# Gated linear attention in a two-layer decoder trunk: where four groups of small products stand in TensorE's queue, and where one scan stands in VectorE's

## The chip, the cores and the metric

The kernel runs on one core of one Trainium2 chip. The metric is the device time of one execution in microseconds (us); the lower, the better. The time quoted for a kernel is the median of its runs.

## The reference, cut to what matters

The reference is a causal decoder trunk of two layers on 512 tokens of 1024 features, in float32. Layer 0 mixes tokens by sliding-window attention and a short convolution, layer 1 by chunked gated linear attention (GLA); each layer then has a gated MLP with a convolution and a gated per-layer embedding. The change lies in the mixer of layer 1 alone:

```python
def _gla_mixer(h, w_in, w_gate_up, gate_bias, o_norm, w_out):
    q, k, v, g_lr, og = _split(h @ w_in, GLA_SPLITS)        # 512, 512, 1024, 16, 1024 columns
    log_a = log_sigmoid(g_lr @ w_gate_up + gate_bias) / 16
    o = _gla_chunked(heads(q) * 128 ** -0.5, heads(k), heads(v), heads(log_a))   # 4 heads, keys 128, values 256
    o = _rms_norm(o, o_norm) * silu(heads(og))
    return o.reshape(b, s, 1024) @ w_out

# within a head, for t >= s:  score[t, s] = sum_d q[t, d] k[s, d] exp(G[t, d] - G[s, d]),  G = cumsum(log_a)
# output[t] = sum_s score[t, s] v[s]
...
```

## The kernel before, in words

Everything is laid out with features or keys on the 128 partitions and the 512 tokens along the free dimension, or, for the values, with 128 tokens on the partitions. There are two kinds of product on TensorE.

The **large products** are the projections with `gla_w_in`. `mm3` (L159 to L165) computes one float32 product out of three with float32r parts: high times high, high times low, low times high. `weights` and `cut` (L118 to L145) load a block of weights and split it: ScalarE rounds it into `wh` (L143), VectorE subtracts to get the rest `wl` (L144). A feature of 128 columns takes 8 x 3 = 24 products of 512 columns into one PSUM bank named `ps`, of which there are four. `query(w, h)`, `key(w, h)` and `gate(w, m)` each make one such feature, and VectorE then copies it out of the bank with a multiplication (L1672, L1680, L1685). A class `Values` makes the values in two steps of 48 products of 336 or 352 columns.

The **small products** are what the attention itself needs, in plain float32, and go to four banks named `pa`. For each head `h`, in order:

- `base(h)`: the scan on VectorE that makes the running sum `G` (L1759), and a multiply of even keys and queries (L1765); GpSimd clears the scores `sc`.
- `diag(h)`: the diagonal, one product with ones (L1771), multiplied into `sc` by VectorE (L1772).
- `decay(h, levels)`, `decay_pairs(h)`, `decay_off(h)`: VectorE and ScalarE make the decay factors `F` of seven block sizes.
- `level(h, levels)`: the scores of each block size (L1806, L1809), merged into `sc` by VectorE; `lo` is the first four sizes, `hi` the fifth; `level_pairs(h)` the last two (L1844).
- `off(h)`: transposes for what passes from block to block (L1888); `state(h)`: the states (L1902), summed by VectorE (L1905).
- `read(h)`: the outputs (L1926, L1928), their squares on ScalarE (L1932), the power -1/2 on GpSimd (L173), and the scaling into `sc` by four multiplies on VectorE (L1936).
- `turn(h)`: eight transposes of the scaled rows (L1943), copied to `oT` by ScalarE (L1947). `gated(m)` then multiplies with the gate.

`load_vectors_ffn(1)` loads small vectors for the next MLP and transposes them with two products (L223).

The order is made in two steps. The program calls these functions in an order written out by hand at the end of `mixer1`; a planner then puts the instructions of each engine into one queue, by that order as priority and by when it expects their inputs. Small products are ready or not at their own times, so the planner puts them between, or in the middle of, the 24 products of a feature. Each engine works through its queue in order: an instruction that waits holds up all that stands behind it. `tc.issue_after(x)` ties what is written in its block, on `x`'s engine alone, to a place behind `x` in that queue; it adds no wait at run time.

In the built queue of before, `diag(0)` is a run of its own between `key(1)` and `query(2)`; `level(0, hi)` and `off(0)` are a run between `query(3)` and `key(2)`, and `level_pairs(0)` with `diag(1)` one between `key(2)` and `key(3)`. From `gate(w, 1)` on there are: `turn(1)` with the two transposes of vectors; `level(3, hi)` after 2 products of `gate(w, 2)`; `off(3)` after 4 more; `read(2)` with `level_pairs(3)` after 4 more; `turn(2)` with `state(3)` after the other 14; `read(3)` after the 24 products of `gate(w, 3)`.

Of the kernel before, what the change touches and what calls it, by code (L numbers as in the profile page):

```python
# [9 lines left out]
F32 = mybir.dt.float32  # L10
# [4 lines left out]
ALU = mybir.AluOpType  # L15
# [3 lines left out]
P = 128  # L19
# [3 lines left out]
ND = D // P  # L23
# [33 lines left out]
class Kernel:  # L57
# [69 lines left out]
    def cut(self, rv, by, at=(0, 0)):  # L127

        nc = self.nc
        na, nb = rv.shape[1:]  # L130
        parts = []
        n = 2 if na * nb > 1024 else 1
        for k in range(n):
            if by == "b":
                a, b = na, nb // n
                v = rv[:, :, k * b : (k + 1) * b]
            else:
                a, b = na // n, nb
                v = rv[:, k * a : (k + 1) * a, :]
            h, l = self.wide("wh", at[0]), self.wide("wl", at[1])  # L140
            hv = h[:, : a * b].rearrange("p (a b) -> p a b", b=b)
            lv = l[:, : a * b].rearrange("p (a b) -> p a b", b=b)
            nc.scalar.activation(hv, v, AF.Copy)  # L143
            nc.vector.tensor_tensor(lv, v, hv.bitcast(F32), ALU.subtract)  # L144
            parts.append((hv, lv))  # L145

        def get(i, c0, c1):
            if by == "b":
                b = nb // n
                k = c0 // b  # L150
                h, l = parts[k]
                return h[:, i, c0 - k * b : c1 - k * b], l[:, i, c0 - k * b : c1 - k * b]
            a = na // n
            h, l = parts[i // a]
            return h[:, i % a, c0:c1], l[:, i % a, c0:c1]

        return get

    def mm3(self, out, lt, rt, start, stop, **kw):  # L159

        mm = self.nc.tensor.matmul
        (lh, ll), (rh, rl) = lt, rt
        mm(out, lh, rh, start=start, stop=False, **kw)  # L163
        mm(out, lh, rl, start=False, stop=False, **kw)  # L164
        mm(out, ll, rh, start=False, stop=stop, **kw)  # L165

    def rsqrt(self, out, src, scale):

# [1455 lines left out]
    def mixer1(self):  # L1624
# [4 lines left out]
        with tc.tile_pool(name="m1", bufs=1) as mp:  # L1629
# [5 lines left out]
            class Values:  # L1635


                def __init__(v, c0, c1, vn):
                    v.c0, v.n, v.vn = c0, c1 - c0, vn
                    v.ws = [  # L1640
                        self.weights(w_in[:, k0 : k0 + 4, 1024 + c0 : 1024 + c1], 4, v.n, by="a") for k0 in (0, 4)
                    ]

                def step(v, i):
                    c0, n, vn = v.c0, v.n, v.vn
                    if i == 0:
                        v.pss = [self.ps() for _ in range(NT)]
                    for k in range(4 * i, 4 * i + 4):
                        for t in range(NT):
                            self.mm3(  # L1650
                                v.pss[t][:, :n], tok(k, t), v.ws[i](k % 4, 0, n), start=k == 0, stop=k == ND - 1
                            )
                    for t in range(NT if i else 0):
                        rt = r[:, t : t + 1]
                        if n > vn:
                            nc.scalar.activation(glr[:, t, :], v.pss[t][:, vn:n], AF.Copy, scale=rt)
                        nc.scalar.activation(vt[t][:, c0 : c0 + vn], v.pss[t][:, :vn], AF.Copy, scale=rt)
# [5 lines left out]

            def feature(w, c):
                ps = self.ps()
                for k in range(ND):
                    self.mm3(ps, w(k, c * P, (c + 1) * P), xg[k], start=k == 0, stop=k == ND - 1)
                return ps

            def query(w, h):  # L1670
                o = qT[h] = self.fp.tile([P, S], F32, tag="a0", name=self.nm("qT"))
                nc.vector.scalar_tensor_tensor(  # L1672
                    out=o, in0=feature(w, h % 2), scalar=float(GDK**-0.5), in1=R, op0=ALU.mult, op1=ALU.mult
                )
# [81 lines left out]
            def base(h):  # L1756

                G = Gs[h] = mp.tile([P, S], F32, tag="G", name=self.nm("G"), bufs=2)
                nc.vector.tensor_tensor_scan(  # L1759
                    G, run.rearrange("p a b -> p (a b)"), las[h], 0.0, op0=ALU.mult, op1=ALU.add  # L1760
                )
                sc = scores[h] = mp.tile([P, GDV * NT], F32, tag="sc", name=self.nm("sc"), bufs=3)

                pr = Fs[h, "diag"] = new()[:, : S // 2]
                nc.vector.tensor_tensor(pr, ev(kT[h]), ev(qT[h]), ALU.mult)  # L1765
                nc.gpsimd.memset(sc[:, :S], 0.0)

            def diag(h):
                sc = scores[h]
                pd = self.pa()[:, : S // 2]  # L1770
                mm(pd, self.ones, Fs[h, "diag"], start=True, stop=True)  # L1771
                nc.vector.tensor_tensor(  # L1772
                    sc[:, :S].rearrange("p (a n b) -> p a n b", a=NT, b=2)[:, :, :, 0],
                    pd.rearrange("p (a n) -> p a n", a=NT),
                    ev(self.ident).unsqueeze(1).to_broadcast([P, NT, P // 2]), ALU.mult,
                )
# [18 lines left out]
            def level(h, levels):  # L1795
                A = scores[h][:, :S]
                for l in levels:
                    b, F = LEVELS[l], Fs[h, l]
                    pl = self.pa()
                    for t in range(NT):  # L1800
                        c = slice(t * P, (t + 1) * P)
                        if b < 64:

                            for u in (0, 64):
                                d = slice(t * P + u, t * P + u + 64)
                                mm(second(pl[u : u + 64, d], b), F[:, d], second(F[:, d], b), start=True, stop=True)  # L1806
                        else:
                            mid = t * P + b
                            mm(pl[:b, mid : mid + b], F[:, t * P : mid], F[:, mid : mid + b], start=True, stop=True)  # L1809
                    if b < 64:  # L1810
                        for u in (0, 64):
                            r = slice(u, u + 64)
                            tv = lambda x: x.rearrange("p (t c) -> p t c", c=P)[r, :, r].rearrange(
                                "p t (n b) -> p t n b", b=2 * b
                            )[:, :, :, b:]
                            mk = second(msk[r, l, r], b).unsqueeze(1).to_broadcast([64, NT, 32 // b, b])
                            nc.vector.copy_predicated(tv(A), mk, tv(pl))
                    else:
                        nc.vector.tensor_copy(second(A[:b], b), second(pl[:b], b))
# [63 lines left out]
            def off(h):  # L1883

                Es, Ec, tot = Fs[h, "off"]
                pt = self.pa()
                for i in range(NT - 1):
                    nc.tensor.transpose(pt[:, i * P : (i + 1) * P], Es[:, i * P : (i + 1) * P], self.ident)  # L1888
                kt = new()
                nc.scalar.copy(kt[:, : 3 * P], pt[:, : 3 * P])  # L1890
                Fs[h, "kt"] = kt
# [46 lines left out]
            def turn(h):  # L1938
                o = scores[h]
                for m in range(2):  # L1940
                    pb = self.pa()
                    for t in range(NT):
                        nc.tensor.transpose(  # L1943
                            pb[:, t * P : (t + 1) * P], o[:, t * GDV + m * P : t * GDV + (m + 1) * P], self.ident
                        )
                    y = self.fp.tile([P, S], F32, tag="a1", name=self.nm("oT"))
                    nc.scalar.activation(y, pb, AF.Copy, scale=self.g_o[:, m : m + 1])  # L1947
                    oT[2 * h + m] = y
# [21 lines left out]
            key(w, 1)  # L1970
            w = pair_w(256)
            base(0)
            diag(0)
            decay(0, lo)
            query(w, 2)
            level(0, lo)
            decay(0, hi)
            decay_off(0)
            decay_pairs(0)
            query(w, 3)  # L1980
            w = pair_w(768)
            level(0, hi)
            off(0)
            base(1)
            decay(1, lo)
            key(w, 2)
            level_pairs(0)
            diag(1)
            key(w, 3)
            v = Values(0, 336, 336)  # L1990
            level(1, lo)
# [3 lines left out]
            v.step(0)  # L1995
            level(1, hi)
            off(1)
            base(2)
            decay(2, lo)
            v.step(1)  # L2000
            v = Values(336, 672, 336)
# [24 lines left out]
            decay_pairs(3)  # L2026
            state(2)
            gate(w, 1)
            turn(1)
            w = pair_w(2064 + 256)  # L2030
            self.load_vectors_ffn(1)
            level(3, hi)
            off(3)
            read(2)
            level_pairs(3)
            gate(w, 2)
            turn(2)
            state(3)
            gated(0)
# [52 lines left out]
```

## Time and profile before

| what | value |
|---|---|
| time, median of 3 runs | 1203.48 us (1203.18 to 1203.55) |
| the profiled execution's own time | 1202.58 us |
| its span, first to last instruction | 1200.8 us |
| TensorE busy with products | 1192.9 us, 99% |
| VectorE busy | 994.2 us, 83% |
| ScalarE busy | 685.2 us, 57% |
| GpSimd busy | 42.9 us, 4% |
| mean granted clock of TensorE | 0.999 |

In the profile PE is TensorE with its products, PEld its weight loads, DVE VectorE, ACT ScalarE, POOL GpSimd. A row of a timeline gives start and duration in us, engine, line, operation, output and inputs; in brackets stands the time that the engine was idle before it and whom it waited for. Products overlap, so the time that one costs is read from the start of one to the start of the next. The stretch of the change reaches from about 615 to 735 us.

### The profile page before, as it was taken

What the parts mean: (1) busy time and instruction counts of PE and PEld (TensorE: products, weight loads), DVE (VectorE), ACT (ScalarE), POOL (GpSimd) and SP (SyncE); (2) the same over time, 40 slices, a digit from 0 to 9 for tenths busy, and PEclk for the clock granted to TensorE, in tenths of its full rate; (3) what the DMA queues carried; (4) which work ended last, traced back from release to release, by engine and by line L of the source; (5) the groups of instructions that cost most, each with busy time, mean ns of one, the idle gap of its engine ahead of it and who ended that gap; (6) DMA issues with size and microseconds to landing.
All of it is one profiled execution on the core that took longest, in us unless ns stands there. A gap on an engine that the chain in (4) does not pass through costs nothing.

```text
span 1200.8 us, 17976 instructions
## 1 busy us (share of the span) xinstructions
PE 1192.9 (99%) x7121; PEld 1038.1 (86%) x7121; DVE 994.2 (83%) x1571; ACT 685.2 (57%) x1116; POOL 42.9 (4%) x64
## 2 busy tenths in 40 slices
PE   9999999999999999999999999999999999999998
PEld 8877788999899889888988988889999999889887
DVE  6886587899999996779769876677999999986895
ACT  7566465656565744566563564555555656644764
POOL 2600000000000000000100000000000000000000
PEclk9999999999999999999999999999999999999999
DMA  7221322323233343331422222313242423422501
GB/s 223 91 88 39 93 83 70 128 84 110 101 101 111 106 141 97 97 106 61 135 73 67 75 71 70 106 43 133 71 141 71 137 75 117 138 88 97 211 1 70
DMA packets 110856, 117.62 MB, mean 98 GB/s; under 512 B 2824, under 2 KB 105794, under 8 KB 110772
## 3 DMA queue, kind: packets, MB, share of 16 engines
q1 hardware_dynamic: 109936, 115.88, 29.6%
q8 instruction: 56, 0.92, 0.3%
q0 software_dynamic: 560, 0.42, 0.3%
q14 instruction: 28, 0.23, 0.1%
q10 hardware_dynamic: 276, 0.18, 0.1%
HBM read 114.37 MB, written 2.10 MB: 97 GB/s over the span
## 4 chain that ended last, share of the span: by engine, by line
PE 89%; DVE 6%; ACT 2%; issue 1%; POOL 1%; DMA 0%; SPq 0%; ACTq 0%; DVEq 0%; POOLq 0%
PE ps L163 11%; PE ps L164 11%; PE ps L165 11%; PE pa L163 7%; PE pa L164 7%; PE pa L165 7%; PE ps L881 6%; PE ps L883 6%; PE ps L882 6%; PE pa L881 2%; PE pa L883 2%; PE pa L882 2%; DVE wl L144 1%; PE ps L1488 1%; PE ps L1486 1%
## 5 line engine op out<-in xcount | busy, mean ns | idle before, releaser
L143 ACT ACTIVATE wh<-raw 128x1024 fp32r<-128x1024 f32 (+4 forms) x144 | 143.7, 998 | 114.3 <-PE ps L164 64.7
L144 DVE TENSOR_TENSOR wl<-raw,wh 128x1024 fp32r<-128x1024 f32 (+4 forms) x144 | 165.8, 1151 | 35.9 <-ACT wh L143 35.1
L828 ACT ACTIVATE wh<-raw 128x1024 fp32r<-128x1024 f32 x84 | 89.2, 1062 | 121.0 <-DVE raw L853 65.2
L941 DVE SCALAR_TENSOR_TENSOR zt<-z,vfa,zt 128x510 f32<-128x510 f32 (+1 forms) x176 | 130.7, 745 | 5.3 <-ACT zt L939 4.7
L829 DVE TENSOR_TENSOR wl<-raw,wh 128x1024 fp32r<-128x1024 f32 x84 | 102.6, 1222 | 20.5 <-ACT wh L828 20.5
L939 ACT ACTIVATE zt<-z,vfb 128x512 f32<-128x512 f32 x88 | 71.0, 809 | 21.0 <-DVE four L992 8.3
L163 PE MATMUL ps<-b,wh 128*128 128x512 f32 x192 | 76.7, 400 | 0.0
L164 PE MATMUL ps<-b,wh 128*128 128x512 f32 x192 | 75.1, 391 | 0.0
L165 PE MATMUL ps<-b,wl 128*128 128x512 f32 x192 | 75.0, 391 | 0.0
L881 PE MATMUL ps<-four,wh 128*128 128x256 f32 x256 | 71.6, 280 | 0.7 <-ACT ps L906 0.7
L883 PE MATMUL ps<-four,wl 128*128 128x256 f32 x256 | 71.0, 277 | 0.0
L882 PE MATMUL ps<-four,wh 128*128 128x256 f32 x256 | 70.8, 277 | 0.0
L164 PE MATMUL pa<-a,wh 128*128 128x512 f32 x176 | 69.0, 392 | 0.0
L164 PE MATMUL pa<-b,wh 128*128 128x512 f32 x176 | 69.0, 392 | 0.0
L163 PE MATMUL pa<-a,wh 128*128 128x512 f32 x176 | 69.0, 392 | 0.0
L163 PE MATMUL pa<-b,wh 128*128 128x512 f32 x176 | 69.0, 392 | 0.0
L165 PE MATMUL pa<-a,wl 128*128 128x512 f32 x176 | 68.4, 389 | 0.0
L165 PE MATMUL pa<-b,wl 128*128 128x512 f32 x176 | 68.4, 389 | 0.0
L881 PEld LDWEIGHTS ps<-four,wh 128*128 128x128 f32 x256 | 48.0, 188 | 3.2 <-ACT ps L906 1.6
L163 PE MATMUL ps<-a,wh 128*128 128x512 f32 x128 | 50.6, 395 | 0.0
L163 PE MATMUL ps<-uh,wh 128*128 128x512 f32 x128 | 50.3, 393 | 0.0
L164 PE MATMUL ps<-a,wh 128*128 128x512 f32 x128 | 50.2, 392 | 0.0
(489 smaller groups left out, 3597.3 us busy)
## 6 DMA issues: line engine op xcount, KB each, us to landing
raw<-in_ffn_w_up_dram SPq DMA_DIRECT2D x44, 1024.0 KB, 5.0
raw<-in_ffn_w_down_dram SPq DMA_DIRECT2D x12, 1024.0 KB, 5.2
raw<-in_hy_w_in_dram SPq DMA_DIRECT2D x8, 1024.0 KB, 5.2
raw<-in_gla_w_in_dram SPq DMA_DIRECT2D x8, 1024.0 KB, 5.2
raw<-in_ffn_w_down_dram SPq DMA_DIRECT2D x8, 768.0 KB, 4.4
raw<-in_ple_w_gate_dram SPq DMA_DIRECT2D x6, 1024.0 KB, 5.1
raw<-in_hy_w_out_dram SPq DMA_DIRECT2D x16, 256.0 KB, 4.1
zt<-in_ffn_w_down_dram SPq DMA_DIRECT2D x8, 512.0 KB, 3.7
```

Source lines behind the costliest of these rows:

```text
L143: nc.scalar.activation(hv, v, AF.Copy)
L144: nc.vector.tensor_tensor(lv, v, hv.bitcast(F32), ALU.subtract)
L163: mm(out, lh, rh, start=start, stop=False, **kw)
L164: mm(out, lh, rl, start=False, stop=False, **kw)
L165: mm(out, ll, rh, start=False, stop=stop, **kw)
L828: nc.scalar.activation(h, src, AF.Copy)
L829: nc.vector.tensor_tensor(l, src, h.bitcast(F32), ALU.subtract)
L881: mm(out, wh, xh, start=first and j == 0, stop=False, **kw)
L882: mm(out, wh, xl, start=False, stop=False, **kw)
L883: mm(out, wl, xh, start=False, stop=j == ND // 2 - 1, **kw)
L939: nc.scalar.activation(y, z, AF.Identity, scale=w2[:, f : f + 1], bias=bb[:, f : f + 1])
L941: nc.vector.scalar_tensor_tensor(out=y[:, tap:], in0=z[:, : S - tap], scalar=w[:, f : f + 1], in1=y[:, tap:], op0=ALU.mult, op1=ALU.add,)
```

## The change

`cut` keeps its last VectorE instruction, `mm3` returns its last product, and `Values` and `feature` keep them in `v.rest` and `products`. `behind(k)` is an `issue_after` of the k-th product of the feature made last. With these, `diag(0)` is written after `query(w, 2)` and tied to a place behind its last product; `level(0, hi)`, `off(0)`, `level_pairs(0)` and `diag(1)` are tied behind `key(w, 2)`; the third head's `base(2)` is tied on VectorE behind the last rest of `Values(0, 336, 336)`; and `turn(1)`, `level(3, hi)`, `off(3)`, `read(2)` and `level_pairs(3)` are written after `gate(w, 2)` and tied behind its fourth group of three products. No instruction is added or taken away on VectorE, ScalarE, GpSimd or the sync queue, and no product on TensorE.

```diff
@@ cut
-            nc.vector.tensor_tensor(lv, v, hv.bitcast(F32), ALU.subtract)
+            self.rest = nc.vector.tensor_tensor(lv, v, hv.bitcast(F32), ALU.subtract)
@@ mm3
-        mm(out, ll, rh, start=False, stop=stop, **kw)
+        return mm(out, ll, rh, start=False, stop=stop, **kw)
@@ Values
+                    v.rest = self.rest.ins
...
+                    products.clear()
...
-                            self.mm3(
-                                v.pss[t][:, :n], tok(k, t), v.ws[i](k % 4, 0, n), start=k == 0, stop=k == ND - 1
+                            products.append(
+                                self.mm3(
+                                    v.pss[t][:, :n], tok(k, t), v.ws[i](k % 4, 0, n), start=k == 0, stop=k == ND - 1
+                                )
                             )
@@ feature
+                products.clear()
                 for k in range(ND):
-                    self.mm3(ps, w(k, c * P, (c + 1) * P), xg[k], start=k == 0, stop=k == ND - 1)
+                    products.append(
+                        self.mm3(ps, w(k, c * P, (c + 1) * P), xg[k], start=k == 0, stop=k == ND - 1)
+                    )
                 return ps
+
+            products = []
+
+            def behind(k=-1):
+                return tc.issue_after(products[k].ins)
@@ the order
             base(0)
-            diag(0)
             decay(0, lo)
             query(w, 2)
+            with behind():
+                diag(0)
             level(0, lo)
             decay(0, hi)
             decay_off(0)
             decay_pairs(0)
             query(w, 3)
             w = pair_w(768)
-            level(0, hi)
-            off(0)
             base(1)
             decay(1, lo)
             key(w, 2)
-            level_pairs(0)
-            diag(1)
+            with behind():
+                level(0, hi)
+                off(0)
+                level_pairs(0)
+                diag(1)
             key(w, 3)
...
             off(1)
-            base(2)
+            with tc.issue_after(v.rest):
+                base(2)
             decay(2, lo)
...
             gate(w, 1)
-            turn(1)
             w = pair_w(2064 + 256)
             self.load_vectors_ffn(1)
-            level(3, hi)
-            off(3)
-            read(2)
-            level_pairs(3)
             gate(w, 2)
+            with behind(3):
+                turn(1)
+                level(3, hi)
+                off(3)
+                read(2)
+                level_pairs(3)
             turn(2)
```

## The prediction

> **What bounds the kernel now.** I read the page first (busy shares, then the chain that ended last), then the waits of TensorE, then the timelines of TensorE, its weight loads and VectorE in the stretches that the change touches. From the page, its span, sections 1 and 4:
>
> ```profile
> span 1200.8 us, 17976 instructions
> PE 1192.9 (99%) x7121; PEld 1038.1 (86%) x7121; DVE 994.2 (83%) x1571; ACT 685.2 (57%) x1116; POOL 42.9 (4%) x64
> PE 89%; DVE 6%; ACT 2%; issue 1%; POOL 1%; DMA 0%; SPq 0%; ACTq 0%; DVEq 0%; POOLq 0%
> ```
>
> TensorE never rests, so every TensorE instruction that takes longer than its share, and every wait on that engine, moves the end by as much. A change of order can gain only two things here: the time lost where the kind of product changes, and TensorE's own waits. The waits of TensorE hold one entry inside the stretch of the change; its place, and what VectorE did then, stand in the two timelines (columns: start in us, duration, engine, line, form):
>
> ```profile
> PE ps L163 <- DVE kT L1680: 0.2, 1, 0.2
> ```
> ```profile
> 651.14 0.43 PE L163 MATMUL ps<-wh,b 128*128 128x336 f32 x1 [0.23 <-DVE kT L1680]
> ```
> ```profile
> 649.15 1.22 DVE L1759 TENSOR_TENSOR_SCAN G<-run,la 128x512 f32<-128x512 f32 x1
> 650.40 0.69 DVE L1680 TENSOR_TENSOR kT<-ps,R 128x512 f32<-128x512 f32 x1
> ...
> 660.39 0.42 DVE L1785 TENSOR_TENSOR F<-G 128x256 f32<-128x256 f32 x1
> ```
>
> The scan of head 2 (the third head) runs 649.15 to 650.37 and pushes back the copy of `key(3)` out of its bank, for which TensorE waits 0.23 us. That scan's own reader comes at 660.39, ten us later.
>
> **Part 1, diag(0) goes behind query(2).** TensorE's timeline around the lone run of `diag(0)`:
>
> ```profile
> 619.85 0.39 PE L165 MATMUL ps<-b,wl 128*128 128x512 f32 x1
> 620.27 0.70 PE L1771 MATMUL pa<-F,ones_r 128*128 128x256 f32 x2
> 620.61 0.58 PE L163 MATMUL ps<-b,wh 128*128 128x512 f32 x1
> 621.03 0.39 PE L164 MATMUL ps<-b,wh 128*128 128x512 f32 x1
> ```
> ```profile
> 724.51 0.39 PE L164 MATMUL ps<-b,wh 128*128 128x512 f32 x1
> ...
> 729.52 0.39 PE L165 MATMUL ps<-b,wl 128*128 128x512 f32 x1
> ```
>
> The second fence gives the step of the large products: 22 of them from 724.51 to 729.52, 0.228 us each. Without the run, 619.85 to 621.03 would be two steps, 0.46; it is 1.18. The run costs 0.73 us, of which its two products take 0.34 (620.27 to 620.61). The other 0.38 is the seam: the way into and out of a run. In the changed queue `diag(0)` stands directly ahead of `level(0, lo)`, which pays its own way in and out already, so 0.38 goes: **-0.38**. On VectorE the multiply that reads `diag`'s bank moves behind query(2)'s copy; the same instructions still stand ahead of the next weights, so nothing else is late.
>
> **Part 2, level(0, hi) and off(0) go behind key(2)**, where `level_pairs(0)` and `diag(1)` stand:
>
> ```profile
> 633.70 0.39 PE L165 MATMUL ps<-b,wl 128*128 128x512 f32 x1
> 634.01 0.66 PE L1806 MATMUL pa<-F 128*64 128x32 f32 x16
> 634.60 0.55 PE L1888 MATMUL pa<-cf,F 128*128 128x128 f32 x3
> 634.91 0.47 PE L163 MATMUL ps<-b,wh 128*128 128x512 f32 x1
> 635.22 0.39 PE L164 MATMUL ps<-b,wh 128*128 128x512 f32 x1
> ```
> ```profile
> 634.01 0.55 PEld L1806 LDWEIGHTS pa<-F 128*64 128x64 f32 x16 [0.35 <-issue]
> ```
>
> 633.70 to 635.22 is 1.52, less two steps 1.07, less the run's own 0.59 and 0.31 leaves a seam of 0.17: **-0.17**. The second fence is the weight load of the same run: it starts with the product (both 634.01), after 0.35 us of rest, so the load was not fetched under the last large product, and that is the way in. The Trainium skill (TensorE: Matmul & The Clock Gate, "Part 2: What happens when you issue a matmul") says that TensorE's queue pulls weight loads ahead of matmuls in flight, and by that rule alone the way in would be hidden and a join would gain only the way out, some 0.08 here. The sum would then come out some 0.1 us later. The trace disagrees at this run, so I go by the row.
>
> `key(2)` now starts right behind `query(3)`, and its third product needs the rounded rest of the weights from VectorE:
>
> ```profile
> 632.83 1.22 DVE L144 TENSOR_TENSOR wl<-raw,wh 128x1024 fp32r<-128x1024 f32 x1
> 633.97 0.42 DVE L1834 TENSOR_TENSOR kT<-kT,F 128x256 f32<-128x256 f32 x1
> ```
>
> TensorE comes to `key(2)` at 634.91 - 1.07 - 0.38 = 633.46 and to its third product at 633.92; the weights are done at about 634.0, since the VectorE instructions ahead of them are the same set. **+0.06** (0 to 0.15).
>
> **Part 3, the scan goes behind the values' weights.** VectorE's instructions issued in `base(2)` (the scan and the first multiply) now stand behind the last `wl` of `Values(0, 336, 336)`; only VectorE's are tied, the clearing of the scores on GpSimd keeps its place. Key(3)'s copy comes 1.22 earlier than 650.40 and the 0.23 on TensorE goes: **-0.23**. Behind the scan now wait head 2's decay differences; they began at 660.39, after the scan of head 3 as well, and VectorE has the same work ahead of them as before, so the scan fits there at no cost. If that cover is gone, the cost is at most the scan's own 1.22 us on the way to `diag(2)`. No DMA of the sync queue changes place.
>
> **Part 4, turn(1) to level_pairs(3) behind gate(2).** Before, five runs (turn(1) with two transposes of loaded vectors; level(3, hi); off(3); read(2) with level_pairs(3); turn(2) with state(3)) lie among the 48 products of gate(2) and gate(3). In the changed queue the two vector transposes stand alone, then 24 products of gate(2), then one run from turn(1) to level_pairs(3), then only 6 products of gate(3), and turn(2) cut in three, with 2 and 1 products between its pieces, state(3), and 15 products. TensorE's rows of before, and then the VectorE group that turn(2) waits for:
>
> ```profile
> 710.28 0.39 PE L165 MATMUL ps<-b,wl 128*128 128x512 f32 x1
> 710.51 1.03 PE L1943 MATMUL pa<-cf,sc 128*128 128x128 f32 x8
> 711.39 0.32 PE L223 MATMUL pa<-cf,vrow 88*128 88x88 f32 x2
> 711.49 0.48 PE L163 MATMUL ps<-b,wh 128*128 128x512 f32 x1
> 711.81 0.40 PE L164 MATMUL ps<-b,wh 128*128 128x512 f32 x1
> ```
> ```profile
> 715.05 1.02 PE L1926 MATMUL pa<-vt,sc 128*128 128x256 f32 x4
> ...
> 717.64 0.59 PE L1928 MATMUL pa<-st,F 128*128 128x256 f32 x2
> 718.17 0.69 PE L1844 MATMUL pa<-qT,kT 128*64 128x64 f32 x16
> 718.78 0.50 PE L164 MATMUL ps<-b,wh 128*128 128x512 f32 x1
> ...
> 722.12 1.03 PE L1943 MATMUL pa<-cf,sc 128*128 128x128 f32 x8
> ```
> ```profile
> 729.75 0.59 PE L1926 MATMUL pa<-vt,sc 128*128 128x256 f32 x2
> ```
> ```profile
> 720.56 1.66 DVE L1936 TENSOR_SCALAR sc<-pa,rq 128x256 f32<-128x256 f32 x4 [0.75 <-POOL rq L173]
> ```
>
> On before's clock from 710.28: vector transposes at 710.51, 0.10; first product of gate(2) 710.61, second 710.93 (the 0.32 of 711.49 to 711.81), 24th 710.93 + 22 x 0.228 = 715.94; turn(1) 716.17, 0.88; level 0.59, off 0.31 (both from part 2); read(2) at 717.95. Its last pair is 2.59 later (715.05 to 717.64), 720.54; level_pairs 3.12 after its start, 721.07, 0.61; then six products, 721.68, 721.99 and four steps, 722.90; TensorE is at turn(2) at **723.13**. Turn(2) needs the scaled rows. Before, their scaling (squares on ScalarE, a power on GpSimd, four multiplies on VectorE) began 2.92 after the last pair (717.64 to 720.56), and the first of four took 1.66 / 4 = 0.42. So the first row is ready at 720.54 + 2.92 + 0.42 = **723.88**: TensorE, which takes its queue in order, waits 0.75 us with gate(3) behind it. Before, 14 products and the pairs covered that (turn(2) at 722.12, no wait); now six do. The later rows come 0.42 apart and the products between the pieces cover those.
>
> From the wait's end: turn(2), state(3) and one product 724.51 - 722.12 = 2.39, two more ways out of 0.09 (0.32 less a step) for the cuts, and 17 products, 3.87: read(3) at 723.88 + 6.44 = 730.32 against 729.75: **+0.57**. Without the wait it would be -0.18. ScalarE's copies of turn(1) now stand behind the rounding of gate(5)'s weights, and read(2)'s banks come free from those copies, about when TensorE gets there; I take 0, up to +0.1. State(3)'s sums on VectorE now have 15 products, 15 x 0.228 = 3.4 us, ahead of read(3) instead of 24, 5.5 us; before showed no wait there, and I take 0, up to +0.3.
>
> **Sum**: -0.38 - 0.17 + 0.06 - 0.23 + 0.57 = -0.15 us. On the profiled execution, 1202.58 (span 1200.8 and 1.8 around it): 1202.4. The median of the runs is 0.9 above that execution: 1203.48 - 0.15 = **1203.3**. About 0.2%, 2.4 us, is what a measurement of this kernel can tell from no change; no term here comes near it.
>
> **The rivals.** (a) No wait at turn(2), because the scaling is quicker with ScalarE's copies of turn(1) done by then and less else in the queues: -0.15 - 0.75 = -0.9, 1202.6. Against it: in the row above VectorE already rested 0.75 us ahead of the multiplies, for GpSimd, so an emptier VectorE shortens nothing. (b) The other side, slower: the wait at turn(2) is longer. Read(1) took longer from its last pair to its multiplies,
>
> ```profile
> 703.98 0.59 PE L1928 MATMUL pa<-st,F 128*128 128x256 f32 x2
> ```
> ```profile
> 707.35 1.66 DVE L1936 TENSOR_SCALAR sc<-pa,rq 128x256 f32<-128x256 f32 x4 [1.12 <-POOL rq L173]
> ```
>
> 3.37 instead of 2.92. Then the sum is -0.15 + 0.45 = +0.3, 1203.8. It is slower than before as soon as the wait passes 0.75 + 0.15 = 0.9 us, and slower by over 0.2% only past 3.3, for which no row speaks. (c) The seam belongs to each small product's own weight load and goes along with it, so that parts 1 and 2 gain nothing: -0.15 + 0.55 = +0.4, 1203.9. Against it: between level and off (634.01, 16 products, 634.60) no load shows a rest. (d) The edit does nothing, because the planner would have put these runs there anyway: the built queues differ as told, so this is nearly excluded.
>
> **Chances.** Forecast 0.50; (a) 0.14, (b) 0.10, (c) 0.07, (d) 0.02, all within 0.2%; together 0.83. Something I don't see, in a stretch where the order of three engines shifts: faster by over 0.2% 0.07, slower by over 0.2% 0.10 (an in-order queue that waits loses more easily than it gains). The range: below, (a) with some 0.6 more for seams that vanish inside the long run and the spread of the runs, 1202.0; above, (b) and (c) together (+0.45 and +0.55 on the forecast) with 0.4 for the banks and for state(3), 1204.7, and a little of the spread, 1204.8.
>
> **What would show it.** TensorE's timeline: `diag` right behind query(2) with no way out of 0.42; level, off, pairs and diag in one run behind key(2); no wait for `kT` L1692 in the waits of TensorE; a new wait of TensorE or its weight loads for VectorE's `sc` of 0.5 to 1.1 us at the first transpose of turn(2). The prediction is wrong if a wait over 1.5 us stands in this stretch, if read(3) starts more than 1 us from before's 729.75, or if the time after 740 us moves by itself.

## The result, and the profile after

The changed kernel takes 1204.64 us in the median (1203.35 to 1207.11, 14 runs), the kernel before in the same sitting 1203.07 us (1202.25 to 1203.85, 14 runs). The ratio is 1.0015, with a 95% interval of 1.0008 to 1.0022: slower, by something between 1.0 and 2.6 us. The time lies in the range that was given, but the sum behind it said -0.15 us.

From the page of the changed kernel, its span and the busy shares:

```profile
span 1202.1 us, 17979 instructions
PE 1193.1 (99%) x7121; PEld 1039.0 (86%) x7121; DVE 994.5 (83%) x1571; ACT 685.8 (57%) x1116; POOL 42.9 (4%) x64
```

The span is 1.3 us longer, and TensorE's busy time only 0.2. TensorE waits more. Its waits in the changed kernel, the three longest (engine, line, whom it waited for: us in total, times, longest):

```profile
PE pa L199 <- DVE mhalf L187: 1.3, 1, 1.3
PE pa L1818 <- DVE sc L1784: 1.1, 1, 1.1
PE pa L1955 <- DVE sc L1948: 0.8, 1, 0.8
```

The first lies ahead of the change and stands in every kernel here. The third, at `turn(2)`, was forecast. The second was not: a product of `level(0, lo)` (L1818) waits for the multiply of `diag(0)` (L1784), and the wait for `kT` is gone.

Times that differ by 1 in 1000 hardly tell versions apart, but TensorE can be used as a clock. The large products are the same in all kernels, so I number them from one ahead of the change and compare when the same one starts. TensorE's timeline of before, with the 1st of them, the 121st (after `level(0, lo)`), the 193rd (after `level(1, lo)`), the 217th (after the wait for `kT`) and the 481st (after `read(3)`), and then the same five of the changed kernel:

```profile
597.11 0.40 PE L165 MATMUL ps<-b,wl 128*128 128x512 f32 x1
...
628.92 0.40 PE L165 MATMUL ps<-b,wl 128*128 128x512 f32 x1
...
649.67 0.32 PE L165 MATMUL ps<-wh,b 128*128 128x336 f32 x1
...
653.87 0.32 PE L165 MATMUL ps<-wh,b 128*128 128x336 f32 x1
...
733.23 0.39 PE L165 MATMUL ps<-b,wl 128*128 128x512 f32 x1
```
```profile
596.97 0.40 PE L165 MATMUL ps<-b,wl 128*128 128x512 f32 x1
...
629.82 0.40 PE L165 MATMUL ps<-b,wl 128*128 128x512 f32 x1
...
650.55 0.32 PE L165 MATMUL ps<-wh,b 128*128 128x336 f32 x1
...
654.23 0.32 PE L165 MATMUL ps<-wh,b 128*128 128x336 f32 x1
...
734.46 0.39 PE L165 MATMUL ps<-b,wl 128*128 128x512 f32 x1
```

From the first row on, before reaches the 121st after 31.81 us, the 193rd after 52.56, the 217th after 56.76, the 481st after 136.12; the changed kernel after 32.85, 53.58, 57.26 and 137.49. The differences grow by +1.04, -0.02, -0.52 and +0.87 us from mark to mark: these are the prices of parts 1, 2, 3 and 4. They add up to +1.37, which lies inside the measured interval. The span grew by 0.1 less, because the first mark itself came 0.14 earlier in the changed kernel (596.97 against 597.11). The same reckoning for every kernel that was run, in us against before:

| kernel | part 1 | part 2 | part 3 | part 4 | sum |
|---|---|---|---|---|---|
| forecast | -0.38 | -0.11 | -0.23 | +0.57 | -0.15 |
| the change | +1.04 | -0.02 | -0.52 | +0.87 | +1.37 |
| e1_diag_bank | -0.32 | +0.08 | -0.43 | +0.85 | +0.18 |
| e8_diag_soon | -0.33 | +0.01 | -0.52 | +0.92 | +0.08 |
| e3_scan_only | 0.00 | +0.01 | -0.52 | +0.04 | -0.47 |
| e4_tail_only | -0.02 | +0.01 | -0.03 | +0.86 | +0.82 |
| e5_turn_late | +1.05 | -0.03 | -0.52 | +0.83 | +1.33 |
| e12_mid | +1.03 | -0.03 | -0.52 | +0.67 | +1.15 |
| e13_best | -0.31 | +0.03 | -0.37 | +0.65 | 0.00 |
| e6_best | -0.30 | +0.03 | -0.42 | 0.00 | -0.69 |
| e15_soon_no_tail | -0.31 | +0.01 | -0.52 | +0.07 | -0.75 |

Where a part is as in before, the entry is within 0.07 of zero; that is how far the reckoning can be trusted. Each row comes from one profiled execution. The first mark, ahead of which nothing was changed, lies between 596.34 (e15) and 597.58 (e6), so the spans of two kernels can differ by over 1 us for reasons outside the stretch, and the marks are compared in their place.

The place of part 1 in the changed kernel, on TensorE:

```profile
625.18 0.39 PE L165 MATMUL ps<-b,wl 128*128 128x512 f32 x1
625.41 0.59 PE L1783 MATMUL pa<-F,ones_r 128*128 128x256 f32 x2
625.93 0.62 PE L1821 MATMUL pa<-F 128*64 128x64 f32 x7
...
626.41 1.10 PE L1818 MATMUL pa<-F 128*64 128x32 f32 x31
628.66 0.66 PE L1818 MATMUL pa<-F 128*64 128x32 f32 x16 [1.15 <-DVE sc L1784]
629.25 0.50 PE L163 MATMUL ps<-b,wh 128*128 128x512 f32 x1
```

and on VectorE at the same time (a choice of rows from a queue without a gap):

```profile
625.62 0.41 DVE L1797 TENSOR_TENSOR F<-G 128x256 f32<-128x256 f32 x1
...
627.17 0.41 DVE L1804 TENSOR_TENSOR F<-F,kT 128x256 f32<-128x256 f32 x1
627.51 0.67 DVE L1684 SCALAR_TENSOR_TENSOR qT<-ps,R 128x512 f32<-128x512 f32 x1
628.11 0.41 DVE L1784 TENSOR_TENSOR sc<-pa,cf 128x256 f32<-128x256 f32 x1
```

The seam ahead of `diag(0)` is short, as forecast: its products start one step of 0.23 after the last large one. But the run now makes five tiles, one of `diag` and four of `level(0, lo)`, and there are four `pa` banks. The last 16 products of `level` want the bank of `diag`, whose products (from 625.41, 0.59 long) end about 626.0. The multiply that empties it stands in VectorE's queue behind the decay factors of the fifth size and of `off`, and behind the copy of `qT`, and starts at 628.11; it is done at 628.52, and at 628.66 TensorE goes on.

The weight loads show a second thing about this seam. The load of `diag` in before, and the loads of `diag` and of `level` in the changed kernel:

```profile
620.26 0.30 PEld L1771 LDWEIGHTS pa<-F,ones_r 128*128 128x128 f32 x2 [0.45 <-DVE F L1765]
```
```profile
625.18 0.41 PEld L1783 LDWEIGHTS pa<-F,ones_r 128*128 128x128 f32 x2
625.93 0.54 PEld L1821 LDWEIGHTS pa<-F 128*64 128x64 f32 x8 [0.33 <-issue]
```

In before `diag` waited for its factors `F`, which VectorE had ready at 620.22 (L1765, 619.82 and 0.40 long). That wait is the whole way in: 619.85 to 620.27 is 0.42, a step is 0.23, so 0.19 of the 0.38 that the prediction called a seam was a wait for VectorE. In the changed kernel the factors are long there, and the load starts under the last large product. The way into `level` did not go: from `diag` to `level` (625.41 to 625.93) pass 0.52 us, 0.18 more than the 0.34 of `diag`'s two products, where in before the way in behind a large product cost 0.09 (626.05 to 626.37, less a step). What remains is 0.19 for the wait, 0.19 for the way out of `diag` (620.61 to 621.03, less a step), 0.09 less 0.18 for the way into `level`: a gain of 0.29, if nothing waited for the bank.

The place of part 2 in the changed kernel, on TensorE:

```profile
640.36 0.66 PE L1818 MATMUL pa<-F 128*64 128x32 f32 x16
640.95 0.55 PE L1900 MATMUL pa<-cf,F 128*128 128x128 f32 x3
641.42 0.69 PE L1856 MATMUL pa<-qT,kT 128*64 128x64 f32 x16
642.04 0.70 PE L1783 MATMUL pa<-F,ones_r 128*128 128x256 f32 x2
642.39 0.58 PE L163 MATMUL ps<-b,wh 128*128 128x512 f32 x1
```

From `off` to `level_pairs` (640.95 to 641.42) pass 0.47 us, where before a large product followed `off` after 0.31. So the seam that was to go stands inside the run, 0.16 us of it; the weight load of `level_pairs` rests 0.17 there (641.42).

The place of part 3 in the changed kernel, on TensorE (the products of 336 columns go on at their step of 0.15 to 0.16), and then the weight load and the neighbours of the wait in before:

```profile
651.01 0.32 PE L165 MATMUL ps<-wh,b 128*128 128x336 f32 x1
...
651.32 0.32 PE L164 MATMUL ps<-wl,b 128*128 128x336 f32 x1
```
```profile
650.60 0.32 PE L165 MATMUL ps<-wh,b 128*128 128x336 f32 x1
...
651.41 0.33 PE L164 MATMUL ps<-wl,b 128*128 128x336 f32 x1
```
```profile
651.14 0.19 PEld L163 LDWEIGHTS ps<-wh,b 128*128 128x128 f32 x1 [0.51 <-DVE kT L1680]
```

Over two steps from one L165 to the L164 behind it: 651.32 - 651.01 = 0.31 after, 651.41 - 650.60 = 0.81 before. The wait cost 0.50 us, about the idle time in the row of the weight load (0.51), and twice the 0.23 in the row of the product.

The place of part 4 in the changed kernel, on TensorE and on VectorE:

```profile
710.67 0.39 PE L165 MATMUL ps<-b,wl 128*128 128x512 f32 x1
...
721.09 0.59 PE L1940 MATMUL pa<-st,F 128*128 128x256 f32 x2
...
723.50 0.39 PE L165 MATMUL ps<-b,wl 128*128 128x512 f32 x1
724.65 0.30 PE L1955 MATMUL pa<-cf,sc 128*128 128x128 f32 x1 [0.76 <-DVE sc L1948]
...
730.99 1.02 PE L1938 MATMUL pa<-vt,sc 128*128 128x256 f32 x4
```
```profile
724.02 1.66 DVE L1948 TENSOR_SCALAR sc<-pa,rq 128x256 f32<-128x256 f32 x4 [0.76 <-POOL rq L173]
```

The scaling begins 2.93 us after the last pair of `read(2)` (721.09 to 724.02; forecast 2.92), and the first transpose of `turn(2)` waits 0.76 by its row. By starts it waits longer: one step after 723.50 it could have begun at 723.73, and it began at 724.65, so 0.92. From 710.67 to `read(3)` it is 20.32 us, before 19.47 (710.28 to 729.75).

### The profile page after: what moved, and what is told of

Its sections match the earlier page's. It is cut to its first block, busy times and chain, and to the rows that moved or that the text cites. A ratio compares the mean times of both kernels' runs of the same rounds, so it can differ in the third digit from the quotient of the medians.

```text
span 1202.1 us, 17979 instructions
## 1 busy us (share of the span) xinstructions
PE 1193.1 (99%) x7121; PEld 1039.0 (86%) x7121; DVE 994.5 (83%) x1571; ACT 685.8 (57%) x1116; POOL 42.9 (4%) x64
## 4 chain that ended last, share of the span: by engine, by line
PE 90%; DVE 5%; ACT 2%; issue 1%; POOL 1%; DMA 1%; DVEq 0%; ACTq 0%; POOLq 0%
PE ps L163 12%; PE ps L164 12%; PE ps L165 11%; PE pa L164 7%; PE pa L163 7%; PE pa L165 7%; PE ps L881 6%; PE ps L883 6%; PE ps L882 6%; PE pa L881 2%; PE pa L883 2%; PE pa L882 2%; DVE wl L144 1%; PE ps L1488 1%; PE ps L1486 1%; PE ps L1487 1%
## 5 line engine op out<-in xcount | busy, mean ns | idle before, releaser
L164 PE MATMUL ps<-b,wh 128*128 128x512 f32 x192 | 75.0, 391 | 0.0
L165 PE MATMUL ps<-b,wl 128*128 128x512 f32 x192 | 75.0, 390 | 0.0
L164 PE MATMUL pa<-a,wh 128*128 128x512 f32 x176 | 69.0, 392 | 0.0
L164 PE MATMUL pa<-b,wh 128*128 128x512 f32 x176 | 69.0, 392 | 0.0
L165 PE MATMUL pa<-b,wl 128*128 128x512 f32 x176 | 68.4, 389 | 0.0
L165 PE MATMUL pa<-a,wl 128*128 128x512 f32 x176 | 68.4, 389 | 0.0
L164 PE MATMUL ps<-a,wh 128*128 128x512 f32 x128 | 50.2, 392 | 0.0
```

The costliest lines, as they stand in the source:

```text
L165: return mm(out, ll, rh, start=False, stop=stop, **kw)
```

## The experiments

Two questions were open: whether the bank is the whole of part 1's loss, and whether each other part is worth what its marks say when it stands alone. Edits are against the changed kernel unless said. The times (each against the kernel before in the same sitting) have intervals of some 0.09% to either side, about 1.1 us, so the verdicts rest on the marks and waits.

**diag's tile gets a bank of its own**, from the four `ps` banks:

```diff
-            def diag(h):
+            def diag(h, bank=self.pa):
...
-                pd = self.pa()[:, : S // 2]
+                pd = bank()[:, : S // 2]
...
-                diag(0)
+                diag(0, self.ps)
```

> The changed kernel, but diag(0) takes its bank from the four of the features (ps) and not from the four of the small products (pa). Bank theory: in the changed kernel the joined run diag(0), level(0, lo) needs five pa banks and has four, so the fourth size's 16 products wait 1.15 us until VectorE has emptied diag's bank; with a bank of its own that wait goes, and the kernel is 1.15 to 1.4 us quicker than the changed one, some 0.1 to 0.3 us above the kernel before. Factor theory (the fourth size's decay factors come late, whatever the bank): the wait of about 1.1 us stays at the same products and so does the time. Seam theory (joining itself costs, not a wait): no wait either way, time as the changed kernel's.

Measured: 1203.53 us against 1202.89, ratio 1.0005 (0.9996 to 1.0014); span 1201.2. TensorE's timeline of this kernel at part 1 and at `key(2)`'s third product, and the row of that product's weight load:

```profile
625.73 0.59 PE L1783 MATMUL ps<-F,ones_r 128*128 128x256 f32 x2
626.26 0.62 PE L1821 MATMUL pa<-F 128*64 128x64 f32 x7
...
626.74 1.57 PE L1818 MATMUL pa<-F 128*64 128x32 f32 x47
628.24 0.51 PE L163 MATMUL ps<-b,wh 128*128 128x512 f32 x1
...
634.31 0.45 PE L165 MATMUL ps<-b,wl 128*128 128x512 f32 x1
634.60 0.40 PE L163 MATMUL ps<-b,wh 128*128 128x512 f32 x1
```
```profile
634.26 0.19 PEld L165 LDWEIGHTS ps<-b,wl 128*128 128x128 f32 x1 [0.22 <-DVE wl L144]
```

All 47 products run through, and part 1 gives -0.32 instead of +1.04. The bank was the whole loss. From the first of these products to the next large one it is 1.50 us (626.74 to 628.24), in the changed kernel 2.84 (626.41 to 629.25): by starts the wait cost 1.34, more than the 1.15 in its row. TensorE now reaches `key(2)` 1.36 us earlier than in the changed kernel, and there the wait for the weights appears that was forecast at +0.06; part 2 comes out 0.10 later than in the changed kernel.

**The bank stays, its emptier goes ahead**: on VectorE, the decay factors, weights and scan that are written behind `diag(0)` are tied behind its multiply, which `diag` now returns.

```diff
             with behind():
-                diag(0)
+                emptied = diag(0)
             level(0, lo)
-            decay(0, hi)
-            decay_off(0)
+            with tc.issue_after(emptied.ins):
+                decay(0, hi)
+                decay_off(0)
...
-            w = pair_w(768)
-            base(1)
+            with tc.issue_after(emptied.ins):
+                w = pair_w(768)
+                base(1)
```

> The changed kernel, diag(0) in a pa bank as there, but on VectorE the decays of the fifth size and of off, the next weights' rest and the next head's scan are tied behind the multiply that empties diag's bank, so that it runs some 1.9 us earlier. Bank theory: what the fourth size's products wait for is this multiply's place in VectorE's queue; moved ahead, the bank is free at about 626.7 on the changed kernel's clock while TensorE comes at 627.5, so the 1.15 us wait goes with four banks as well, the mark behind level(0, lo) falls by about 1.3 us and the time by 1.1 to 1.4 under the changed kernel. Rival (four banks are too few for the joined run whatever VectorE does): a wait of some 0.5 us or more stays at the fourth size.

Measured: 1203.35 us against 1202.80, ratio 1.0005 (0.9996 to 1.0014); span 1201.1. TensorE's and VectorE's timelines of this kernel at part 1:

```profile
626.61 1.57 PE L1818 MATMUL pa<-F 128*64 128x32 f32 x47
```
```profile
625.84 0.69 DVE L1684 SCALAR_TENSOR_TENSOR qT<-ps,R 128x512 f32<-128x512 f32 x1
626.44 0.43 DVE L1784 TENSOR_TENSOR sc<-pa,cf 128x256 f32<-128x256 f32 x1
```

With four banks again, and the multiply at 626.44 instead of 628.11, no product waits: -0.33. So either repair does, more banks or an earlier emptier; what hurt in the change was the two together, five tiles for four banks and the emptier late in its queue.

The wait for the weights of `key(2)` is not in this kernel, although TensorE is as early as in e1. The planner put two products ahead of `key(2)`, at 633.73 and 633.95, which belong to the feature behind it (their third, L165, follows at 641.74 behind the run), so that `key(2)`'s third product comes at 634.63 and finds its weights. In e15 below it is the same. Part 2 stands there without that wait, and it gives +0.01.

**Part 3 alone**: the kernel before, with only the scan moved.

```diff
-            base(2)
+            with tc.issue_after(v.rest):
+                base(2)
```

> The kernel before with part 3 alone: the third head's scan behind the values' weights. If the wait for key(3)'s copy is worth what the weight load's row says (0.51 us of rest), the stretch from level(1, lo) to off(1) on TensorE shortens by 0.5 us (8.96 to about 8.45) and the time goes to 0.5 under the kernel before; if it is worth what the product's row says (0.23), the stretch shortens by 0.23. If the later scan holds up head 2's decay, a new wait shows before level(2, lo) and takes the gain back.

Measured: 1202.54 us, ratio 0.9997 (0.9987 to 1.0006); span 1200.0. By the marks -0.52 at the 217th product and nothing given back by the 481st (+0.04): the scan costs nothing at its new place, and the gain is twice the forecast's 0.23.

**Part 4 alone**: the kernel before, with `turn(1)` to `level_pairs(3)` under `with behind(3):` after `gate(w, 2)`.

> The kernel before with part 4 alone: turn(1) to level_pairs(3) behind gate(2). Wait theory: the 0.75 us wait of TensorE at the first transpose of turn(2) shows here as well, and gate(2)'s first products to read(3) take 0.85 us longer than before (20.3 instead of 19.5 us); the time is 0.85 above the kernel before. Rival (all of the loss is diag's bank and part 4 is even): the stretch takes 19.5 us and the time is the kernel before's.

Measured: 1203.86 us, ratio 1.0006 (0.9997 to 1.0016); span 1201.5. The first transpose of `turn(2)` in TensorE's timeline of this kernel:

```profile
723.96 0.30 PE L1955 MATMUL pa<-cf,sc 128*128 128x128 f32 x1 [0.76 <-DVE sc L1948]
```

The same wait and the same price as in the whole change, +0.86 against +0.87: part 4 doesn't depend on the others.

**turn(2) moved behind the products of gate(3)**, so that it can't wait. It is tied behind their fifth group and was queued behind all of them; `state(3)` now follows `level_pairs(3)` directly:

```diff
-            turn(2)
             state(3)
             gated(0)
             gated(1)
             gate(w, 3)
+            with behind(4):
+                turn(2)
```

> The changed kernel with turn(2) tied behind the fifth group of gate(3)'s products and state(3) ahead of it. Wait theory: the wait at turn(2) goes, and with the cuts of turn(2) gone as well the stretch from the last product of gate(1) to read(3) falls from 20.3 to about 19.2 us; the time is about 1.1 under the changed kernel, the bank wait at level(0, lo) of 1.15 stays. Rival (the wait moves on): turn(2) or read(3) or the third product of state(3) shows a new wait of some 0.5 us and the stretch stays above 19.8 us.

Measured: 1204.35 us, ratio 1.0012 (1.0003 to 1.0022); span 1202.6. The wait is not at `turn(2)` any more; TensorE's timeline of this kernel shows where it is:

```profile
725.53 0.70 PE L1914 MATMUL pa<-vt,F 128*128 128x256 f32 x2 [0.66 <-DVE sc L1948]
```

L1914 is `state(3)`: its third pair of products needs a bank of `read(2)`, and that bank comes free by the same scaling L1948. Part 4 stays at +0.83: the wait moved from one reader of the scaling's work to another. The edit brought `state(3)` closer to `read(2)`, so this doesn't show that the place of `turn(2)` is without effect; a kernel with both of them late was not run.

**More cover**: the run stands behind 12 products of gate(2) instead of 24, so that 12 follow it.

```diff
-            with behind(3):
+            with tc.high_priority(offset=150), behind(3):
                 turn(1)
```

> The changed kernel with the long run of part 4 raised in priority, so that it stands in the middle of gate(2), 12 products in, and turn(2), in one piece, behind the other 12. Cover theory (the wait at turn(2) is a matter of how many products stand between read(2) and turn(2)): 12 products and the pairs, 0.6 + 2.8 us, cover the 3.3 us from the last pair to the first scaled row, so no wait at turn(2), and gate(1)'s end to read(3) takes some 0.2 us less than the kernel before (19.3; the changed kernel 20.3). Rival (the run of seven banks with four costs by itself): a wait for ScalarE's copies of turn(1) of 0.3 us or more shows at read(2), or level_pairs waits, and the stretch stays above 19.5.

Measured: 1204.05 us, ratio 1.0010 (1.0001 to 1.0019); span 1202.2. TensorE's and VectorE's timelines of this kernel at `turn(2)` and `state(3)`:

```profile
722.15 1.40 PE L1955 MATMUL pa<-cf,sc 128*128 128x128 f32 x8
723.39 1.03 PE L1914 MATMUL pa<-vt,F 128*128 128x256 f32 x4
724.57 0.67 PE L1914 MATMUL pa<-vt,F 128*128 128x256 f32 x2 [0.15 <-DVE sc L1867]
```
```profile
721.07 1.66 DVE L1948 TENSOR_SCALAR sc<-pa,rq 128x256 f32<-128x256 f32 x4 [0.76 <-POOL rq L173]
```

The wait of 0.76 is gone, but part 4 still costs +0.67. `turn(2)` starts 1.08 us after the scaling and takes 1.24 to the next kind of product, where it took 0.88 before (the forecast's figure for eight transposes): the transposes come faster than the rows, 0.42 apart, and wait on the way (the weight loads of L1955 rest 0.25 for L1948 at 722.79). Then `state(3)` waits for a bank again, now that of `level_pairs(3)` (L1867). Twelve products and the pairs, 4.00 us from the start of the last pair of `read(2)` (718.15) to `turn(2)`, are not enough cover for the chain of 2.93 and four rows; in before it was 14 products and the pairs, 4.48 (717.64 to 722.12).

**Three versions put together from the parts.** e13_best is e1_diag_bank with e12_mid's edit and part 2 undone; e6_best is e1_diag_bank with parts 2 and 4 undone; e15_soon_no_tail is e8_diag_soon with part 4 undone.

> The kernel before with diag(0) behind query(2) in a bank of its own (ps), the scan behind the values' weights, and part 4 in the middle of gate(2); part 2 left out. If the parts add: -0.32 - 0.5 - 0.2 = -1.0 us against the kernel before, ratio 0.9992; no wait of TensorE for VectorE between 600 and 740 us. If they do not add, because the copy of key(3) or the weights of key(2) come late again, -0.5 or less and a wait at key(2)'s third product.

> The same without part 4: diag(0) in a bank of its own and the scan. -0.32 - 0.5 = -0.8 us against the kernel before if the two add; part 4 in the middle of gate(2) is worth the difference of this run and the one with it, 0.2 us by the cover theory, 0 or a loss by its rival.

> The kernel with diag's multiply moved ahead on VectorE, and parts 2 and 3, but without part 4. If part 4 is a loss of 0.85 us wherever it stands and nothing else differs, TensorE's mark at the end of the stretch lies 0.8 us ahead of the kernel before (0.82 was reached there ahead of part 4 in the run with it), and the time 0.8 under before, ratio about 0.9993. Rival: without part 4 a wait that was hidden behind it shows between read(2) and turn(2), and the mark lies 0.3 us ahead or less.

Measured: e13_best 1202.86 us, ratio 1.0001 (0.9992 to 1.0010); e6_best 1202.46, ratio 0.9995 (0.9987 to 1.0004); e15_soon_no_tail 1202.03 against 1202.75, ratio 0.9995 (0.9986 to 1.0004). By the marks the last two are 0.69 and 0.75 us ahead of before, about what was expected of them (0.8). That is 0.06%, which the times don't separate from zero: both lie below before in the median, and their intervals take in 1. e15 has the shortest span of all, 1199.4, but of the 1.4 us that it lies below before's, 0.8 were there at the first mark already (596.34 against 597.11). e13 was expected at -1.0 and came out at 0.00, because part 4 in the middle of `gate(2)`, counted there as a gain of 0.2, costs 0.65, which is nearly all that parts e13 from e6.

In e1, e6 and e13 part 3 gives a little less than 0.52 (0.43, 0.42 and 0.37). What is missing stands at one place: the steps to the large product that waited for `kT` in before, the 200th, and to the one behind it are 0.15 and 0.23 in e1, 0.15 and 0.25 in e6, 0.19 and 0.26 in e13, and 0.15 both times in the changed kernel. In e13 the weight load there waits 0.16 for `kT`; in e1 and e6 no row names a releaser, so that it is the same copy, ending at 650.64 in e1, is likely and not shown.

## Why the prediction was wrong

**Part 1 is the step that failed**, by 1.42 us (-0.38 forecast, +1.04 measured), and without it the sum would have been near zero (e1 +0.18, e8 +0.08). The sentence that failed is the last of that part: the multiply that reads `diag`'s bank moves behind query(2)'s copy, "so nothing else is late". It asked who waits for the multiply's result, and the answer to that was right. It didn't ask who waits for the bank that the multiply reads. As a run of its own, `diag` had its bank emptied (L1772, done at 623.15) long before `level` came at 626.37; directly ahead of `level` it takes one bank of four from a run that needs four. The term of -0.38 itself comes out near, -0.32 and -0.33 where the wait is taken away, but that owes something to luck: 0.19 of it was `diag`'s wait for VectorE, which the prediction read as the way into a run, and the way into `level` stayed. The list of TensorE's waits, from which the prediction worked, shows the products' waits alone; this one stands in the row of the weight load.

**Part 2** was forecast at -0.17 for the seam and +0.06 for the wait for weights; measured -0.02. Of the seam, 0.16 came back between `off` and `level_pairs`, so joining gained nothing, nor did it in e8 (+0.01), where no wait for weights stands. The wait didn't show in the changed kernel, because part 1 made TensorE late; in e1 it shows, and there it costs 0.06: the products around it start at 634.31 and 634.60, 0.29 apart instead of 0.23. The working took the weights as done at about 634.0; its own row gives 634.05 (632.83 and 1.22), by which the wait would have been 0.13. Rival (c), a seam that belongs to a small product's own weight load and goes along with it, holds here: the load of `level_pairs` rests behind `off` too. Against it the prediction set that no load rests between `level` and `off`, but the loads of `off` are 128 columns wide, and those of `level` and `level_pairs`, which rest, 64. In part 1 the way into `level` stayed likewise (0.33 of rest), and what went was `diag`'s wait and its way out.

**Part 3** had the right mechanism and a term that was too small, 0.23 for 0.52. The 0.23 came from the idle time in the product's row, which counts from the modelled end of the product ahead. The Trainium skill (Perfetto Trace Analysis, "Tensor Engine Instruction (MATMUL, LD_WEIGHTS)") says that the profiler works out a TensorE end from the instruction's size and doesn't observe it. The trace agrees: by starts alone the wait cost 0.50, by the modelled end 0.23. In e3, with nothing else moved, the gain is 0.52.

**Part 4** had the right mechanism: the wait stands where it was forecast, and the chain behind it is 2.93 long for 2.92. The price is 0.3 too small. The row's 0.76 only seems to meet the forecast's 0.75: the forecast reckoned from start to start, and reckoned so the wait is 0.92. `read(2)`'s last pair came 0.16 later in the stretch than forecast (721.09 - 710.67 = 10.42, against 10.26), which is two seams inside the joined run: `turn(1)` to `level` took 0.97 (716.56 to 717.53) and not 0.88, `off` to `read(2)` 0.38 (718.12 to 718.50) and not 0.31. From the scaling's start the first row takes 0.42, to 724.44, and the transpose begins at 724.65, so handing it over takes 0.21 that the forecast left out. From there on it was 0.10 quicker than forecast (6.34 for 6.44). Rival (a), no wait, is excluded by the wait's row; rival (b), a chain of 3.37, by the chain of 2.93. Moving the wait (e5) or covering it (e12) gave back 0.04 and 0.20 of 0.87, so in both most of it stays; undone (e6, e15), it goes. ScalarE's copies and `state(3)`'s sums, for which the forecast left up to 0.4, show no wait on TensorE.

Of the prediction's signs of being wrong one came: `read(3)` starts at 730.99, 1.24 us from before's 729.75. The signs that the mechanisms work came too: no wait for `kT`, `diag` right behind `query(2)`, one run behind `key(2)`, and the new wait at `turn(2)`. They don't tell whether the sum is right, because none of them looks at the banks.

That the time lies in the range is luck. Its upper end was made of rivals (b) and (c) and of 0.4 for the banks of `read(2)` and for `state(3)`; the loss came from a bank of which the working says nothing. The chances gave 0.10 to an unseen cost in the in-order queues, but only for over 0.2%. It was of that kind and 0.15%, which 14 runs of each kernel tell from zero, with an interval of 0.07% to either side.

## What to carry to other kernels

Before joining two runs of small products, count the tiles of the joined run against the banks, and look where each bank's emptier stands in its own queue: the emptier that was early enough for two runs can be too late for one. The work that stands between a product and the reader of its result is cover; part 4, which was to save 0.18 us by joining, uncovered a chain of 2.93 and lost 0.87. Before a gap ahead of a run is called a seam, look at the row of its weight load: it may name what the run waits for. Size a wait of TensorE from starts, with and without it. The idle times undersize it in the products' rows (0.23 for 0.50, 1.15 for 1.34, 0.76 for 0.92), and the loads' rows miss to either side (0.51, 1.23 and 1.16 for the same three).

## What the runs showed of the hardware

Whether a run has a way in goes, in these traces, with the width of its weight loads. A load of 128x128 starts under the product ahead of it when its input is there: `diag`'s at 625.18 for a product at 625.41, `turn(1)`'s at 716.34 for one at 716.56. The first load of a run of 128x64 (`level`, `level_pairs`) starts only with its own product, in every one of these runs of before and of the changed kernel between 620 and 740 us, after a rest of 0.35 to 0.40 us behind a product of 512 columns, 0.33 behind one of 256, 0.20 or 0.21 behind one of 336 and 0.17 behind the transposes of 128; the rest is the same whether its row names a releaser or none. So a change from one kind of small product to another can cost as much as a change to the large ones: `off` to `level_pairs` took 0.47 us from start to start inside the run, `off` to a large product 0.31. Joining gave 0.32 of 0.38 for `diag` with `level`, more than half of it from a wait for VectorE that went along, and 0.02 of 0.17 for `off` with `level_pairs`, which is nothing within the 0.07 of the reckoning.
